# A hybrid decoder step with a mixture of experts: rows of second and third expert blocks move without a branch

## The chip, the cores and the metric

One core of a Trainium2 chip runs the whole program. The metric is device microseconds of one execution; a time that is told without more is the median of several runs. Times inside an execution come from a profile of one execution and count from the start of its span.

## The reference

Two trunk layers run over 512 prompt tokens and 64 sample tokens (8 sequences of 8), width 1024. Each layer has a mixer of three recurrences (GLA, retention, SSD) between two projections, a layer norm, and then a mixture of experts, which is where the change lies:

```python
p_group = softmax(t @ w_group + b_group)          # 4 groups
g_sel = argmax(p_group)
e_logits = (t @ w_expert + b_expert)[group g_sel]  # 4 experts in a group
top_v, top_i = top_k(e_logits, 2)
w_top = softmax(top_v) * p_group[g_sel]
hid = silu(t @ w1[e]) * (t @ w3[e])                # 256 wide, 16 experts
y = sum over e of w_top[e] * (hid @ w2[e])
```

Every token has two experts out of sixteen, so a layer has 2 x 576 = 1152 rows to send through experts. How many an expert gets depends on the data, and the kernel must be right for any split.

## The kernel before, in words

**The stage.** In each layer `phase_b` ends with the routing, and `experts` (L1819) then takes the sixteen experts in sixteen *turns*, `b` = 0 to 15, most crowded expert first in rank; the list `RANK` (L34) says which rank is taken in which turn. Every turn's expert gets a main block. A turn is *light* (`LIGHT`, L36: turns 0, 1, 3, 4, 6, 7, 9) when 64 rows are expected to do: class `Light` (L1392) gathers 64 rows and multiplies in plain float32. The other turns have a `Block` (L1307) of up to 128 rows, whose weights and rows are split in two parts (`split`, L323; L328 on ScalarE, L329 on VectorE; L1340, L1341 for the rows) for three products each.

**A block** is: `gather` (L1320, an indirect DMA on GpSimd's queue that fetches the rows of its tokens from `hbuf` by the indices in `srci`; an index past the end, 2047, fetches nothing), `turn` (L1329, eight transposes L1334), `up` (L1343, products L1353, SiLU L1355, L1357), `hid` (L1360), `down` (L1366, products L1373, written to a `ys` tile) and `scatter` (L1379, an indirect DMA L1384 on GpSimd's queue that writes the rows to `ybuf`). In a light block the lines are L1417, L1425, L1434 and L1442.

**More rows than a block has.** An expert of a non-light turn with more than 128 rows has a second block (`b2`), with more than 256 a third (`b3`); a light turn with more than 64 rows has a second light block (`bx`), and above 128 and 256 whole blocks on top; what lies above 384 rows goes through left-over blocks ahead of the turns (L1965, `nx` of them). `counts` (L1202) works this out on VectorE and writes numbers and bit masks to a small tile `ebi`; `values_load` (L1930) puts four of them (`nx`, `second`, `third`, `beyond`) in registers of every engine, and `tc.If` makes a branch on all engines. The body of an `If` is scheduled as one piece. A body that is skipped is replaced by instructions that bring the semaphores to where the body would have left them: an event semaphore on each engine and, where the body holds DMAs of GpSimd's queue, a counter step for these.

**Order of the turns.** The loop at L1988 runs 17 times. In turn b TensorE does `up` of block b, `turn` of block b + 1, `down` of block b - 1 and `hid` of block b. Between them stands one `If` per turn (L2009) on all the cases "at hand", and in it one for each case (`two`, L1906; `three`, L1908): in turn b - 1 the gather of b's second block (L2050), in turn b its transposes, up products and hidden rows (L2035 to L2040) with those of the third block, whose gather is there too, and in turn b + 1 its down products and scatter. The case of a light turn stands whole in its own turn (L2020 to L2032). Fifteen of the seventeen turns have such an `If`. Scatters of the non-light blocks have a branch of GpSimd alone that takes 64 or all rows (`parts`, L1934; L1938), and the gather of turn 9 is put ahead of its turn's branch (`GSPLIT`).

Weights come in pieces of 1 MB (`load`, L1915; DMA L1286 on SyncE's queue), three experts deep; a piece is asked for when the expert that held its room is through. Between the turns GpSimd also normalizes the residual rows (`aside`, L1848; L1854, L1855), once per turn in turns 2 to 6.

Of the kernel before, what the change touches and what calls it, by code (L numbers as in the profile page):

```python
# [9 lines left out]
F32 = mybir.dt.float32  # L10
# [28 lines left out]
ROWS = [min(128, 2 * T // max(r - 1, 1)) for r in RANK]  # L39

HALF = [64 if r > 80 else r for r in ROWS]
GSPLIT, SSPLIT = (9,), tuple(range(NE - 2))
SECOND = [b for b in range(NE) if RANK[b] < 2 + 2 * T // 129]
SOON = (2,)
THIRD = [b for b in range(NE) if RANK[b] < 2 + 2 * T // 257]
# [19 lines left out]
def _tables():  # L65
# [60 lines left out]
    put("pow2", np.tile(2.0 ** np.arange(16), (128, 1)))  # L126
    put("iota256", np.tile(np.arange(256.0), (128, 1)))
# [33 lines left out]
def _body(nc, tc, a, ctx, dbg):  # L161
# [1040 lines left out]
    def counts(tp, R, tabs, perm, count):  # L1202
# [189 lines left out]
    class Light(Block):  # L1392
# [27 lines left out]
        def up(self):  # L1420
# [76 lines left out]
    def phase_b(l, gates, nrm, gst, slots, rqk, rv, x, R, tabs, rst, fill):  # L1497
# [23 lines left out]
        R["iota"] = rp.tile([128, 481], F32, name="iota")  # L1521
        sp.dma_start(R["iota"], a["consts"][:, nres:nres + 481])
# [296 lines left out]
    def experts(last, finish, l, x, R, tabs, slots, rqk, rv, ahead):  # L1819
# [8 lines left out]
        with ExitStack() as sE:  # L1828
# [19 lines left out]
            def aside(b):  # L1848
                if 2 <= b < 2 + NT:
# [3 lines left out]
                    with tc.issue_after(bl[max(k for k in range(min(b + 3, NE)) if k not in GSPLIT)].got.ins):  # L1853
                        pool.tensor_tensor(xt, xt, ln1[:n, 0], op=ALU.mult)  # L1854
                        pool.tensor_tensor(xt, xt, ln1[:n, 1], op=ALU.add)  # L1855
# [36 lines left out]
            def take(t):  # L1892

                n = tp_(t)
                if t not in ys:
# [4 lines left out]
            bx = {b: light(b, Xx[b % 2], psx, 1, yss[3]) for b in LIGHT}  # L1900
            b2 = {b: Block(NE + b, tabs, scat, Xx[b % 2], xf if b in LIGHT else xs, hids[2], yss[3], sl2, psx, plain=b in LIGHT) for b in SECOND}
            b3 = {b: Block(2 * NE + b, tabs, scat, Xx[(b + (b in SOON)) % 2], xf if b in LIGHT else xs, hids[3], yss[(b + 2) % 3], sl2, psx, plain=b in LIGHT)
                  for b in THIRD}

            def two(b):
                return tc.If((beyond & (1 << b)) > 0)  # L1906

            def three(b, f):  # L1908
                if b in THIRD:
                    with tc.If((third & (1 << b)) > 0):  # L1910
                        f()
# [450 lines left out]
```

## Time and profile before

| | |
|---|---|
| median of 3 runs | 1481.08 us (1478.7 to 1485.45) |
| the profiled execution | 1481.09 us |
| its span, first to last instruction | 1479.3 us |
| granted TensorE clock, mean over the span | 0.918 of full speed |
| TensorE busy (matmul) | 1243.2 us, 84% |
| VectorE, ScalarE, GpSimd busy | 816.6, 488.1, 430.4 us (55, 33, 29%) |
| DMA | 267.45 MB, 181 GB/s over the span |
| experts' stage, layer 0 / layer 1 | about 475 to 700 us / 1165 to 1435 us |

An engine's busy time counts only work of the engine itself: branches, register loads, semaphore steps and the issuing of DMAs are not in it. A row of waits says which engine's instruction waited, for what, how long in all, how many times and the longest. "PEq L2009" as the reason means that TensorE's own instruction sequencer was at line 2009, a branch; "issue" means that the profile shows nothing it waited for. "PEldq" in the rows on branches is the same sequencer.

### The profile page before, as it was taken

The numbers are of one execution on the slowest core, as the hardware profiler recorded it, in microseconds if no ns is written. First come the engines' busy times: TensorE is split into PE (matmuls) and PEld (weight loads), VectorE is DVE, ScalarE is ACT, GpSimd is POOL, SyncE is SP. The second block draws the span as 40 slices with busy tenths as digits, with TensorE's granted clock in tenths as the row PEclk, the third lists the DMA queues.
The fourth block names the chain that finished last, engine by engine and source line by source line (L and its number), as shares of the span: only waits on it lengthen the run. The fifth ranks groups of instructions, "written<-read, shape, count | busy, mean of one in ns | idle before, by whom it ended". The sixth has DMA issues, their size and how long they took to land. (4 is left out here: it accounts for less than half of the span.)

```text
span 1479.3 us, 22669 instructions
## 1 busy us (share of the span) xinstructions
PE 1243.2 (84%) x8166; PEld 939.3 (63%) x8166; DVE 816.6 (55%) x1905; ACT 488.1 (33%) x902; POOL 430.4 (29%) x356
## 2 busy tenths in 40 slices
PE   4999999998985685999899998889997478558993
PEld 0998677675763454576589887777576355435761
DVE  0566457446888230366768647336789623022657
ACT  0552133321353221454454223323145223122522
POOL 0014112224153461221242322133324365112115
PEclk9999999999986797999999999999997689789997
DMA  8545666755152746796615310027544273572862
GB/s 293 184 144 164 221 228 212 279 203 184 66 170 91 259 171 230 288 404 240 191 65 171 88 58 33 29 63 271 172 161 136 107 290 124 231 275 95 346 204 90
DMA packets 96018, 267.45 MB, mean 181 GB/s; under 512 B 26263, under 2 KB 54841, under 8 KB 76920
## 3 DMA queue, kind: packets, MB, share of 16 engines
q1 hardware_dynamic: 84600, 246.60, 47.5%
q0 software_dynamic: 11264, 18.87, 3.8%
q8 instruction: 88, 1.44, 0.4%
q14 instruction: 66, 0.54, 0.1%
HBM read 238.43 MB, written 39.24 MB: 188 GB/s over the span
## 5 line engine op out<-in xcount | busy, mean ns | idle before, releaser
L402 PE MATMUL ps<-whi,hT 128*128 128x256 f32 (+1 forms) x640 | 189.9, 297 | 1.8 <-ACT hT L493 1.0
L404 PE MATMUL ps<-whi,hT 128*128 128x256 f32 (+1 forms) x640 | 184.1, 288 | 1.8 <-DVE hT L494 1.7
L403 PE MATMUL ps<-wlo,hT 128*128 128x256 f32 (+1 forms) x640 | 184.4, 288 | 0.7 <-DVE wlo L329 0.7
L402 PEld LDWEIGHTS ps<-whi,hT 128*128 128x128 f32 (+1 forms) x640 | 118.8, 186 | 15.1 <-issue 10.4
L403 PEld LDWEIGHTS ps<-wlo,hT 128*128 128x128 f32 (+1 forms) x640 | 118.5, 185 | 3.4 <-issue 2.1
L404 PEld LDWEIGHTS ps<-whi,hT 128*128 128x128 f32 (+1 forms) x640 | 118.5, 185 | 3.2 <-DVE hT L494 2.4
L392 PE MATMUL ps<-hT,whi 128*128 128x288 f32 x512 | 88.6, 294 | 0.0
L329 DVE TENSOR_TENSOR wlo<-wraw,whi 128x2048 fp32r<-128x2048 f32 x30 | 68.6, 2288 | 33.3 <-ACT whi L328 33.1
L1341 DVE TENSOR_TENSOR xl<-ps,xh 128x512 fp32r<-128x512 f32 x48 | 31.2, 684 | 89.6 <-ACT xh L1340 84.1
L265 PE MATMUL ada<-wada,scond 128*32 128x512 f32 x384 | 58.1, 678 | 21.0 <-DMA wada<-w_ada 21.0
L392 PEld LDWEIGHTS ps<-hT,whi 128*128 128x128 f32 x512 | 74.7, 188 | 0.4 <-ACT zdt L531 0.4
L1562 PE MATMUL ps<-whi,mh 128*128 128x512 f32 (+1 forms) x160 | 70.9, 443 | 3.7 <-ACT mh L1548 3.7
L329 DVE TENSOR_TENSOR wlo<-w3rd,whi 128x2048 fp32r<-128x2048 f32 x22 | 55.2, 2507 | 30.9 <-ACT whi L328 29.7
L1564 PE MATMUL ps<-whi,ml 128*128 128x512 f32 (+1 forms) x160 | 68.3, 431 | 3.8 <-DVE ml L1549 3.8
L1563 PE MATMUL ps<-wlo,mh 128*128 128x512 f32 (+1 forms) x160 | 70.1, 438 | 0.0
L1353 PE MATMUL ps<-whi,xh 128*128 128x256 f32 x384 | 58.9, 298 | 7.6 <-DVE xl L1341 7.6
L328 ACT ACTIVATE whi<-wraw 128x2048 fp32r<-128x2048 f32 x30 | 57.3, 1911 | 19.4 <-PE ps L392 7.7
L842 POOL TENSOR_TENSOR qh<-qx,ex 128x256 f32<-128x256 f32 x32 | 31.3, 1007 | 99.2 <-issue 83.5
L1373 PE MATMUL ps<-w3rd,hid 128*128 128x512 f32 x128 | 58.1, 596 | 2.2 <-DVE ys L1377 2.2
L1353 PEld LDWEIGHTS ps<-whi,xh 128*128 128x128 f32 x384 | 51.6, 199 | 11.5 <-DVE xl L1341 11.0
L1322 POOL DMA_INDIRECT qk<-hbuf,srci x22 | 22.7, 1033 | 121.6 <-PE ps L1417 70.0
L1384 POOL DMA_INDIRECT ybuf<-ys,srci x20 | 27.5, 1375 | 104.4 <-ACTq L2009 33.9
(552 smaller groups left out, 2937.5 us busy)
## 6 DMA issues: line engine op xcount, KB each, us to landing
wada<-w_ada SPq DMA_DIRECT2D x48, 1024.0 KB
wraw<-moe_w SPq DMA_DIRECT2D x36, 1024.0 KB
slots<-moe_w SPq DMA_DIRECT2D x30, 1024.0 KB
w3rd<-moe_w SPq DMA_DIRECT2D x30, 1024.0 KB
wraw<-w_in SPq DMA_DIRECT2D x22, 1024.0 KB
wraw<-w_out SPq DMA_DIRECT2D x8, 1024.0 KB
ybuf<-bz SPq DMA_DIRECT2D x8, 512.0 KB
hbuf<-g SPq DMA_DIRECT2D x8, 512.0 KB
```

The costliest lines, as they stand in the source:

```text
L265: pe.matmul(acc[32 * q:32 * q + 32, :], sc_[:, k, :], w[:, o:o + 512], start=(k == 0), stop=(k == KD - 1))
L328: split.hi = act.activation(hi[:, :n], raw[:, :n], AF.Copy)
L329: dve.tensor_tensor(lo[:, :n], raw[:, :n], hi[:, :n].bitcast(F32), op=ALU.subtract)
L392: pe.matmul(p[:mw, :], lhs[:, k, m0:m0 + mw], rhs[:, k, 288 * h:288 * (h + 1)], start=(k == 0 and lhs is vh and rhs is hT[0]), stop=(k == ...
L402: pe.matmul(p[:n], hT[0][:, k, xs], vh[:, k, :], start=(k == 0), stop=False)
L403: pe.matmul(p[:n], hT[0][:, k, xs], vl[:, k, :], start=False, stop=False)
L404: pe.matmul(p[:n], hT[1][:, k, xs], vh[:, k, :], start=False, stop=(k == KD - 1))
L1353: pe.matmul(p, x[:, k], v[:, k], start=(x is self.xh and v is vh and k == 0), stop=(x is self.xl and k == KD - 1))
L1373: pe.matmul(p, self.hT[:, f], v[:, f, c], start=(f == 0), stop=(f == 1))
L1562: pe.matmul(p[:n], mh[:, k, :n], vh, start=(k == 0), stop=False)
L1563: pe.matmul(p[:n], mh[:, k, :n], vl, start=False, stop=False)
L1564: o = pe.matmul(p[:n], ml[:, k, :n], vh, start=False, stop=(k == 3))
```

## The change

Second and third blocks of the non-light turns (`MORE`: turns 2, 5, 8, 10, 11, 12, 13; a third block in turns 2, 5, 8, 13) are gathered and scattered in any case, outside of any branch; where an expert has too few rows for them, all their indices are past the end. A second block is gathered two turns ahead of its own, a third one turn ahead, and both are scattered in their own turn. Only their products (`extra`) stand behind a branch: one on b's bit, and in it one on the third's. All of a block's work, its down products too, is now in its own turn. The cases of light turns go out of the turns: they stand, with the left-over blocks, in one branch ahead of the loop, which loads its weights itself. One register, `flags`, holds all bits; the others are loaded inside that branch. The extra gathers use two X tiles in turn, `ys` tiles that could be read unwritten are zeroed by VectorE, and the 64-row scatters and the special place of turn 9's gather are gone. Small edits of tables (`pow3`, the width of `iota` and `ebi`) are left out here.

```diff
+MORE = [b for b in SECOND if b not in LIGHT]
+LIGHTS, NXS, THIRDS = sum(1 << b for b in LIGHT), 16, {b: 19 + i for i, b in enumerate(b for b in THIRD if b not in LIGHT)}
...
-        dve.scalar_tensor_tensor(j[:, 3], p, float(min(HALF[:NE - 2])), R["iota"][0:1, 465:481], op0=ALU.is_gt, op1=ALU.mult, accum_out=b[:, 3:4])
         dve.tensor_tensor(j[:, 0], p, R["iota"][0:1, 449:465], op=ALU.is_gt)
-        dve.scalar_tensor_tensor(j[:, 0], j[:, 0], 1.0, R["iota"][0:1, 465:481], op0=ALU.mult, op1=ALU.mult, accum_out=b[:, 4:5])
-        dve.tensor_copy(tabs[2][:, NX + 19:NX + 21], b[:, 3:5])
+        dve.scalar_tensor_tensor(j[:, 0], j[:, 0], 1.0, R["iota"][0:1, 465:481], op0=ALU.mult, op1=ALU.mult, accum_out=b[:, 3:4])
+        dve.scalar_tensor_tensor(j[:, 3], p, 256.0, R["iota"][0:1, 481:497], op0=ALU.is_gt, op1=ALU.mult, accum_out=b[:, 4:5])
+        dve.scalar_tensor_tensor(b[:, 3:4], b[:, 0:1], 2.0 ** NXS, b[:, 3:4], op0=ALU.mult, op1=ALU.add)
+        dve.tensor_tensor(tabs[2][:, NX + 19:NX + 20], b[:, 3:4], b[:, 4:5], op=ALU.add)
...
+            b2, b3, k = {}, {}, 0
+            for b in SECOND:
+                for i, d in enumerate((b2, b3)):
+                    if i == 0 or b in THIRD:
+                        d[b] = Block((1 + i) * NE + b, tabs, scat, Xx[k % 2], xf if b in LIGHT else xs, hids[2 + i], yss[3] if i == 0 else yss[(b + 1) % 3],
+                                     sl2, psx, plain=b in LIGHT)
+                        k += 1
...
-            nx, second, third, beyond = [nc.values_load(tabs[2][0:1, i:i + 1], min_val=0, max_val=m)
-                                         for i, m in ((NX, NX), (NX + 1, 2 ** NE - 1), (NX + 2, 2 ** NE - 1), (NX + 20, 2 ** NE - 1))]
-            half = pool.value_load(tabs[2][0:1, NX + 19:NX + 20], min_val=0, max_val=2 ** NE - 1)
+            flags = nc.values_load(tabs[2][0:1, NX + 19:NX + 20], min_val=0, max_val=2 ** 23)
+
+            def bit(i):
+                return tc.If((flags & (1 << i)) > 0)
+
+            def extra(q, w):
+
+                q.w = w
+                q.turn()
+                for i in range(2):
+                    q.up(i)
+                q.hid()
+                q.down()
...
+            dve.memset(yss[3], 0.0)
+            dve.memset(yss[0][:, 512:], 0.0)
...
-            with tc.If(nx > 0), ExitStack() as sI:
+            with tc.If((flags & (LIGHTS | 7 << NXS)) > 0):
+                for b in LIGHT:
+                    with bit(b):
+                        e = sp.value_load(tabs[2][0:1, NX + 3 + b:NX + 4 + b], min_val=0, max_val=NE - 1)
+                        for i in range(3):
+                            expert_piece(l, e, i, w3rd[i])
+                        whole(bx[b], w3rd)
+                        if b in SECOND:
...
+                nx = nc.values_load(tabs[2][0:1, NX:NX + 1], min_val=0, max_val=NX)
+                wr = w3rd[0]
+                with tc.If(nx > 0), ExitStack() as sI:
...
-                if b + 3 in GSPLIT:
-                    parts(b + 3, bl[b + 3].gather, True)
-
-                at_hand = [e for e in (b - 1, b, b + 1) if e in SECOND and e not in LIGHT or e == b and b in LIGHT]
...
-                with tc.If((beyond & sum(1 << e for e in at_hand)) > 0) if at_hand else nullcontext():
-                    if b - 1 in at_hand:
-                        with two(b - 1):
-                            b2[b - 1].down()
-                            b2[b - 1].scatter()
...
-                    if b in at_hand and b in LIGHT:
-                        with two(b):
...
-                    elif b in at_hand:
-                        with two(b):
-                            b2[b].turn()
-                            if b not in SOON:
-                                three(b, lambda: b3[b].gather())
-                            b2[b].up(0)
-                            b2[b].up(1)
-                            b2[b].hid()
...
-                    if b + 1 in at_hand:
-                        with two(b + 1):
-                            b2[b + 1].gather()
...
+                if b in MORE:
+                    with bit(b):
+                        extra(b2[b], bl[b].w)
+                        if b in THIRD:
+                            with bit(THIRDS[b]):
+                                extra(b3[b], bl[b].w)
...
                 if b + 1 < NE:
                     bl[b + 1].turn()
-                    if b + 3 < NE and b + 3 not in GSPLIT:
+                    if b + 3 < NE:
                         bl[b + 3].gather()
+
+                    for e, d in ((b + 1, b3), (b + 2, b2)):
+                        if e in MORE and e in d:
+                            d[e].gather()
...
-                    st = parts(b - 1, bl[b - 1].scatter, b - 1 in SSPLIT)[0]
+                    st = bl[b - 1].scatter()
+                    for d in (b2, b3):
+                        if b in MORE and b in d:
+                            d[b].scatter()
```

## Rows read from the trace of the kernel before

**Rows 1.** The page, busy us (share of the span) and instructions of TensorE

```profile
PE 1243.2 (84%) x8166; PEld 939.3 (63%) x8166; DVE 816.6 (55%) x1905; ACT 488.1 (33%) x902; POOL 430.4 (29%) x356
```

**Rows 2.** By stage: length, PE PEld DVE ACT POOL busy (instructions), clock, DMA share, GB/s

```profile
475.00:700.00 225.00, 183.82 (x1105) 125.57 (x1106) 86.64 (x109) 76.15 (x105) 72.71 (x50) 0.91 0.70 262
1165.00:1435.00 270.00, 209.81 (x1243) 143.97 (x1244) 88.41 (x117) 77.73 (x113) 77.36 (x52) 0.89 0.58 215
```

**Rows 3.** Waits of TensorE, stage of layer 0: us in total, times, longest

```profile
PE ps L1334 <- DMA X<-hbuf,srci: 13.6, 1, 13.6
PE ps L1334 <- PEq L2020: 5.7, 1, 5.7
PE ps L1417 <- PEq L2009: 5.2, 1, 5.2
PE ps L1442 <- PEq L2020: 3.4, 3, 1.4
```

**Rows 4.** Waits of TensorE, stage of layer 1

```profile
PE ps L1334 <- DMA X<-hbuf,srci: 29.2, 2, 15.4
PE ps L1417 <- PEq L2009: 4.9, 1, 4.9
...
PE ps L1442 <- PEq L2020: 4.1, 4, 1.7
...
PE ps L1334 <- PEq L2020: 1.7, 1, 1.7
```

**Rows 5.** Timeline of GpSimd around 560 us: start, us, instruction, idle before

```profile
555.58 1.03 POOL L1384 DMA_INDIRECT ybuf<-ys,srci  x1 [0.17 <-issue]
566.11 1.02 POOL L1322 DMA_INDIRECT X<-hbuf,srci  x1 [9.50 <-issue]
```

**Rows 6.** GpSimd's sequencer at L2020, 555.6 to 566 us

```profile
L2020 POOLq COMPARE_BRANCH  x1: 45/45/45, 555.7 to 555.7; - x1
L2020 POOLq EVENT_SEMAPHORE  x1: 17/17/17, 564.6 to 564.6; - x1
```

**Rows 7.** Timeline of TensorE, 573 to 588 us

```profile
575.15 1.94 PE L1334 MATMUL ps<-cst,X 128*128 128x128 f32 x8 [13.55 <-DMA X<-hbuf,srci]
577.70 2.07 PE L1353 MATMUL ps<-whi,xh 128*128 128x256 f32 x8 [0.61 <-DVE xl L1341]
...
581.97 1.11 PE L1353 MATMUL ps<-whi,xh 128*128 128x256 f32 x8
```

**Rows 8.** Source lines L1322: gathers into the X tiles, ns min/median/max

```profile
L1322 POOL DMA_INDIRECT X<-hbuf,srci x6: 1004/1028/1033, 502.4 to 1320.1; - x6
```

**Rows 9.** Timeline of TensorE, transposes elsewhere in the stage

```profile
601.10 1.09 PE L1334 MATMUL ps<-cst,v 128*128 128x128 f32 x8
```

**Rows 10.** Table by stretch, columns as in rows 2: just after the X wait

```profile
575.00:581.00 6.00, 5.24 (x24) 4.87 (x25) 1.38 (x2) 1.20 (x2) 0.00 (x0) 0.53 0.04 14
```

**Rows 11.** TensorE's sequencer at L1965, branch of the left-over blocks, both layers

```profile
L1965 PEldq COMPARE_BRANCH  x2: 3860/4164/4467, 487.2 to 1175.1; - x2
```

**Rows 12.** Flag loads of TensorE's sequencer at L1930, ns min/median/max

```profile
L1930 PEldq TENSOR_LOAD <-ebi x8: 300/308/497, 486.6 to 1179.9; - x8
```

**Rows 13.** TensorE's sequencer at L2009 in turn 0 of layer 0

```profile
L2009 PEldq COMPARE_BRANCH  x1: 1929/1929/1929, 493.2 to 493.2; - x1
```

**Rows 14.** All branches of TensorE's sequencer at L2020 and L2009

```profile
L2020 PEldq COMPARE_BRANCH  x15: 170/218/6783, 501.6 to 1364.2; - x15
...
L2009 PEldq COMPARE_BRANCH  x30: 68/148/2428, 493.2 to 1410.6; - x30
```

**Rows 15.** Timeline of TensorE: down products of the last turn, idle before

```profile
693.54 3.70 PE L1373 MATMUL ps<-wraw,hid 128*128 128x512 f32 x8 [0.47 <-ACT hid L1364]
```

**Rows 16.** Source line L1384: scatters, ns min/median/max

```profile
L1384 POOL DMA_INDIRECT ybuf<-ys,srci x20: 973/998/3036, 544.3 to 1418.8; - x20
```

**Rows 17.** Groups of GpSimd: normalized rows, busy and mean ns, idle before

```profile
L1855 POOL TENSOR_TENSOR x<-x,slots 128x1024 f32<-128x1024 f32 (+1 forms) x10 | 29.5, 2948 | 0.8
...
L1854 POOL TENSOR_TENSOR x<-x,slots 128x1024 f32<-128x1024 f32 (+1 forms) x10 | 23.7, 2367 | 0.2
```

More of the change, by code (lines that the diff above doesn't have):

```diff
@@ L126, in _tables @@
     put("pow2", np.tile(2.0 ** np.arange(16), (128, 1)))
+    put("pow3", np.tile([2.0 ** THIRDS[b] if b in THIRDS else 0.0 for b in range(NE)], (128, 1)))
     put("iota256", np.tile(np.arange(256.0), (128, 1)))
@@ L1418, in turn, with up @@
             act.activation(self.xT, p.rearrange("p (k n) -> p k n", k=KD), AF.Copy)
-        def up(self):
+        def up(self, i=0):
             v = [w.rearrange("p (k n) -> p k n", k=KD) for w in self.w[:2]]
@@ L1520, in phase_b @@
         pool.tensor_copy(R["ur"][:, 1], ones)
-        R["iota"] = rp.tile([128, 481], F32, name="iota")
-        sp.dma_start(R["iota"], a["consts"][:, nres:nres + 481])
+        R["iota"] = rp.tile([128, 497], F32, name="iota")
+        sp.dma_start(R["iota"], a["consts"][:, nres:nres + 497])
         wm = rp.tile([128, KD, 2, 20], F32, name="wm")
@@ L1852, in aside @@
                     act.activation(xt, xt, AF.Identity, scale=st[:, 1:2], bias=st[:, 2:3])
-                    with tc.issue_after(bl[max(k for k in range(min(b + 3, NE)) if k not in GSPLIT)].got.ins):
+                    with tc.issue_after(bl[min(b + 2, NE - 1)].got.ins):
                         pool.tensor_tensor(xt, xt, ln1[:n, 0], op=ALU.mult)
@@ L1897, in take @@
                 loads[t] = [sp.dma_start(ys[t][:n, k], ybuf[PL * k + 128 * t:PL * k + 128 * t + n]) for k in range(2)]
[L1900 to L1911, printed above, removed]
+            bx = {b: light(b, Xx[0], psx, 1, yss[3]) for b in LIGHT}
+            b2, b3, k = {}, {}, 0
[5 more added lines that the diff above has]
+                        k += 1
             ids = {0: 0, 1: 1}
@@ L1929, in experts @@
                 pool.memset(ln1[:, i, 0:1], 0.0)
-            nx, second, third, beyond = [nc.values_load(tabs[2][0:1, i:i + 1], min_val=0, max_val=m)
-                                         for i, m in ((NX, NX), (NX + 1, 2 ** NE - 1), (NX + 2, 2 ** NE - 1), (NX + 20, 2 ** NE - 1))]
-            half = pool.value_load(tabs[2][0:1, NX + 19:NX + 20], min_val=0, max_val=2 ** NE - 1)
-            def parts(b, f, both):
-                h, r = HALF[b], ROWS[b]
-                if b not in LIGHT and h < r and both:
-                    with tc.If((half & (1 << b)) > 0) as big:
-                        o = [f(slice(0, r))]
-                    with big.Else():
-                        o.append(f(slice(0, h)))
-                    return o
-                return [f(slice(0, r))]
+            flags = nc.values_load(tabs[2][0:1, NX + 19:NX + 20], min_val=0, max_val=2 ** 23)
[8 more added lines that the diff above has]
+                q.down()
             def whole(q, w):
@@ L1949, in whole @@
                 q.turn()
-                for i in range(2):
+                for i in range(1 if isinstance(q, Light) else 2):
                     q.up(i)
```

74 lines of the change are left out of this document (24 added, 50 removed).

## The prediction

> **What bounds the kernel now.** I read the busy lines first: TensorE is the busy engine [rows 1]. The change touches one stage that runs once per layer, the sixteen turns of the experts, so next comes the table by stage: in the first layer's stage (225 us) TensorE is busy 183.8 us, in the second's (270 us) 209.8, and there the DMA engines stand at 0.70 and 0.58 and GpSimd works 73 and 77 us [rows 2]. So TensorE sets the pace, and some 41 and 60 us of its idle time are what can be won. Third, the waits of TensorE in these stretches [rows 3, 4]. Nearly all are of two kinds: "DMA X", a wait for the gathered rows of a second block (13.6 us once, 29.2 us in two), and "PEq", where TensorE's own sequencer stood in a branch (L2009, L2020).
>
> Why the rows of X come late is seen on GpSimd's queue. It issues a scatter at 555.58 and the X gather at 566.11, with nothing between [rows 5]. In between its sequencer leaves the untaken branch of a 64-row block (L2020) in 45 ns at 555.7, and the next thing it does is a semaphore wait that is over at 564.6 [rows 6]. As I read it, a skipped body that holds GpSimd transfers has to step the counters of the transfers left out, and that waits until an earlier scatter has landed, 9 us after its issue. Only then comes the gather, and its rows need 9.0 us more (566.11 to 575.15 [rows 5, 7]).
>
> **The change, part by part.** Rows in the trace show six extra blocks: six X gathers [rows 8], two in the first layer, four in the second. Their products are in both kernels.
>
> (1) *Gathers out of the branches, two turns ahead (a second block) or one (a third).* GpSimd's list has no counter to step between the turns any more. A gather issued a turn or two ahead of a product that PE reaches 12 us or more per two turns later covers the 9.0 us landing. Gone: 13.6 + 29.2 = 42.8 us. What is late next in turn 5 is the block's down weights: issued a turn before and behind them PE still has some 9 us of the extra block's own up products, so I charge nothing; if that cover were missing it would cost up to the rest of one landing, 9 us, kept for the upper end.
>
> (2) *Clock after these waits.* Right after the wait the eight transposes took 1.94 us against 1.09 elsewhere, the first eight products 2.07 against 1.11 a few lines later [rows 7, 9], and the granted clock of that stretch is 0.53, so mostly the lower of its two levels, after 13.55 us in which TensorE did nothing [rows 7, 10]. 0.85 + 0.96 = 1.8 us, three times: 5.4 us gone.
>
> (3) *Branch of turn 0.* TensorE waits 5.2 and 4.9 us [rows 3, 4]. In that time it skips the left-over blocks (branch of 4.47 and 3.86 us, partly under earlier products [rows 11]), loads three more flags (0.31 us each [rows 12]) and skips the 64-row case of turn 0 (1.93 us [rows 13]). The first stays, now over a longer body; the flags become one, the last goes. 1.93 + 3 x 0.31 = 2.9 us in the first layer; for the second I take 2.6, its wait being 0.3 shorter. 5.5 us. Bounds: if the longer skip costs the dearest branch in the trace, 6.78 us [rows 14], instead of 4.2, it eats 2 x 2.6 = 5.2, so this part is worth 0.3 to 5.5.
>
> (4) *Branch of turn 1.* The skip of its 64-row case, with two whole blocks inside it, is that 6.78 us branch; TensorE waited 5.7 and 1.7 us on it. 7.4 us gone.
>
> (5) *Skips of 64-row cases in later turns* (3, 4, 6, 7, 9): "ps L1442 from PEq L2020", 3.4 and 4.1 us [rows 3, 4]: 7.5 us gone.
>
> (6) *The seven branches left in each layer.* Their bodies are about what the outer branch of such a turn skips now; the 30 of L2009 have a median of 0.15 us and a worst of 2.43 [rows 14]. They are run ahead of the array, so I charge 0; bounds 0 to 14 x 2.43 = 34 us (the worst row in all), and I stay near the median.
>
> (7) *Down products inside the branch.* Today an extra block's down products run a turn later, with its hidden rows long ready. Now they follow directly and wait for them, as in the last turn: 0.47 us [rows 15]. Six times: 3 us added, bounds 0 to 6.
>
> (8) *GpSimd.* 11 gathers and 11 scatters per layer in any case are 44, against 12 today: 32 more at 1.0 us each [rows 8, 16], 18 in the first stage, 14 in the second. GpSimd would work 91 us in each. Nothing waits for it as long as its list of a turn is shorter than the turn; I charge 4 us for a scatter that comes a little late and holds a ys tile (a guess; bounds 0 to rival A). On the DMA engines the absent rows have indices past the end and are dropped; even if all moved, 32 x 0.5 MB are 43 us at 262 / 0.70 = 374 GB/s [rows 2], in room that lies idle.
>
> (9) *Counting, flag arithmetic, two memsets on VectorE, full instead of half scatters, fewer flag loads on SP:* a handful of instructions beside TensorE's work in the head of the stage; the flags are needed only after the transposes of turn 0. 0.
>
> Sum: 42.8 + 5.4 + 5.5 + 7.4 + 7.5 - 3 - 4 = 61.6, or 62 us. The profiled execution took 1481.1 us (span 1479.3), the median of the runs shown is 1481.1 too: 1481 - 62 = **1419 us** (-4.2%).
>
> **Rivals.**
>
> A: *GpSimd falls behind, and the X wait comes back as a wait for its list.* In turns 2 to 6 it also carries the normalized rows, 2.4 + 2.9 us a turn [rows 17]. Turns 2 to 5 have 4, 3, 3 and 4 transfers; 3.5 at 1.0 us and these make 8.8 us, under the 12.5 us of a turn (200 us over 16). But the same scatter has taken up to 3.04 us [rows 16]: at that price 3.5 x 3.04 + 5.3 = 16 us a turn, 3.5 too much in four turns of two layers: 28 us, 1447 us. Against it: the median is 1.0. [...] 0.16.
>
> B: *Other waits fill the place,* the weights above all: TensorE goes through the stage 30 us faster with the same 48 MB. Half of (1) and (2) comes back: 24 us, 1443 us. Against it: DMA share 0.70 and 0.58 [rows 2]. 0.10.
>
> C (slower): *every skip of a second block fetches its code.* A block of the second kind with its third is some 260 TensorE instructions to jump over; (4) shows such a jump at 6.78 us, (3) at 3.86 to 4.47. Place: the 14 branches, on TensorE's sequencer. Price n each: 14 n - 62 us; it decides from n = 4.4 us, and at 5.5 gives +15, 1496 us. Against it: median 0.15 [rows 14]. [...] 0.04.
>
> D: *the change does not do what it says:* the early gathers still wait on GpSimd, for their X tile to be freed in the branch two turns before, and land as late. (1) and (2) stay, 48 us: 1467 us. 0.03.
>
> **How the numbers follow.** The forecast itself has 0.67 with 1400 to 1435 (costs in (7), (8) at zero and some clock won at the head of the stage; or (3) at 0.3, one landing in (1)). The range takes in A and B, 1398 to 1450; C, D and the far ends are left out. About 0.5%, 7.4 us, is what a measurement of this kernel can tell. Faster: forecast, A, B, most of D, 0.94; same 0.03; slower 0.03.
>
> **What would show it.** Right: no "DMA X" among TensorE's waits; X gathers two turns ahead of their transposes, GpSimd with 76 + 32 transfers; no branch wait in turn 1; stages near 200 and 235 us; no half-clock stretch in mid-stage. Wrong: TensorE waiting for xh or ys behind a scatter's landing or GpSimd at work without gaps (A); DMA share near 1 with waits for weights (B); branches of microseconds at the seven skips (C); X waits as before (D).

## The result and the profile after

| | before | after |
|---|---|---|
| median, lowest to highest | 1479.89 us (1478.64 to 1485.45, 4 runs) | 1433.81 us (1431.05 to 1434.84, 4 runs) |
| profiled execution, its span | 1481.09, 1479.3 us | 1432.89, 1431.1 us |
| GpSimd instructions | 356 | 388 |
| experts' stage, layer 0 / layer 1 | 217.7 / 262.4 us | 203.8 / 230.1 us |

The change makes the kernel faster: the ratio is 0.968, 95% interval 0.965 to 0.971, or 46 us where 62 were forecast; 1434 lies in the range. A stage is counted here from the first transposes of turn 0's rows (L1417 before, L1419 after) to the end of the last down product (L1373, L1375). Of the 48 us by which the span is shorter, 13.9 are in the first stage and 32.4 in the second, and the first one starts 3.7 us earlier; 1.7 are lost again outside of the two. In the changed kernel the same code stands one to two lines lower in the file (L1384 is L1386 there, L329 is L330).

TensorE's waits after, by line and reason: total, how many, the longest. First the stage of layer 0 (475 to 680 us), beside [rows 3]:

```profile
PE ps L1355 <- ACT xh L1342: 6.3, 2, 3.3
PE ps L1355 <- DVE wlo L330: 5.0, 1, 5.0
PE ps L1355 <- DVE xl L1343: 4.3, 4, 2.0
PE ps L1419 <- PEq L1963: 2.2, 1, 2.2
...
PE ps L1375 <- ACT hid L1366: 1.4, 3, 0.5
```

then that of layer 1 (1152 to 1383 us), beside [rows 4]:

```profile
PE ps L1355 <- ACT xh L1342: 6.3, 2, 3.3
PE ps L1355 <- DVE xl L1343: 5.9, 6, 1.8
PE ps L1355 <- DVE wlo L330: 4.4, 2, 3.1
...
PE ps L1375 <- ACT hid L1366: 2.4, 5, 0.5
PE ps L1419 <- PEq L1963: 2.0, 1, 2.0
```

No wait for "DMA X" is left, nor one for a branch in turn 1 or in a later 64-row turn; turn 0's branch (now L1963) costs 2.2 and 2.0 us. In their place stand waits that the kernel before does not have: for the split rows (their first part is xh, the second xl) and for the split weights (whi and wlo). They stand in two places. The first is turn 2; TensorE, VectorE and GpSimd there, from three timelines of the changed kernel (start, duration, instruction, and in brackets the idle time before it and what ended it):

```profile
504.18 2.08 PE L1355 MATMUL ps<-wlo,xh 128*128 128x256 f32 x8 [4.96 <-DVE wlo L330]
506.05 1.72 PE L1355 MATMUL ps<-whi,xl 128*128 128x256 f32 x8
507.61 1.11 PE L1355 MATMUL ps<-whi,xh 128*128 128x256 f32 x8
```

```profile
497.21 6.91 DVE L330 TENSOR_TENSOR wlo<-w3rd,whi 128x2048 fp32r<-128x2048 f32 x1 [1.18 <-ACT whi L329]
```

```profile
491.10 1.00 POOL L1324 DMA_INDIRECT X<-hbuf,srci  x1 [0.30 <-issue]
...
497.28 2.39 POOL L1857 TENSOR_TENSOR x<-x,slots 128x1024 f32<-128x1024 f32 x1
499.62 2.35 POOL L1856 TENSOR_TENSOR x<-x,slots 128x1024 f32<-128x1024 f32 x1
502.14 2.93 POOL L1386 DMA_INDIRECT ybuf<-ys,route  x1 [0.17 <-issue]
```

The split takes 6.91 us, and it lies beside two operations of GpSimd on the normalized rows: 2.29 us, what such a split takes elsewhere, and 2.39 and 2.35 make 7.03. The next one, 4.26 us from 505.36 on, lies beside most of a third (2.38 us from 505.08 on). TensorE waits 4.96 us and then runs at about half speed for a while (2.08 and 1.72 us, then 1.11; the granted clock from 503 to 508 us is 0.66). Before the change the same split took 2.29 us, and GpSimd stood idle beside it, from its X gather until TensorE had done the transposes behind turn 1's branch. VectorE and GpSimd in the kernel before:

```profile
505.82 2.29 DVE L329 TENSOR_TENSOR wlo<-w3rd,whi 128x2048 fp32r<-128x2048 f32 x1 [1.19 <-DMA wraw<-moe_w]
...
511.54 1.00 POOL L1322 DMA_INDIRECT v<-hbuf,srci  x1 [8.14 <-PE ps L1334]
```

The second place is turns 11 and 12. TensorE at the end of turn 10:

```profile
608.37 1.94 PE L1444 MATMUL ps<-wraw,hid 128*64 128x512 f32 x8
610.24 0.44 PE L1365 MATMUL ps<-cst,qk 128*128 128x128 f32 x2
613.96 2.07 PE L1355 MATMUL ps<-whi,xh 128*128 128x256 f32 x8 [3.28 <-ACT xh L1342]
615.83 2.04 PE L1355 MATMUL ps<-wlo,xh 128*128 128x256 f32 x8
...
630.29 2.08 PE L1355 MATMUL ps<-whi,xh 128*128 128x256 f32 x8 [3.06 <-ACT xh L1342]
```

and ScalarE:

```profile
610.36 0.69 ACT L1445 ACTIVATE ys<-ps,route 128x512 f32<-128x512 f32 x1 [5.33 <-PE ps L1444]
610.94 0.38 ACT L1366 ACTIVATE hid<-ps 128x256 f32<-128x256 f32 x1
611.51 1.91 ACT L329 ACTIVATE whi<-w3rd 128x2048 fp32r<-128x2048 f32 x1 [0.19 <-ACTq L2016]
613.33 1.07 ACT L1342 ACTIVATE xh<-ps 128x512 fp32r<-128x512 f32 x2
```

ScalarE idles 5.3 us, passes the untaken branch of turn 10 (L2016), and only then splits weights and rows of block 11, with TensorE waiting. The granted clock from 612 to 622 us is 0.66; in steps of half a microsecond it reads 1.00 up to 613.0 us, 0.50 from 613.5 to 620.0 and 1.00 again from 620.5 on:

```profile
612.00:622.00 10.00, 8.04 (x44) 7.98 (x45) 5.69 (x4) 4.58 (x5) 4.02 (x3) 0.66 0.97 377
```

(its columns: stretch, length, busy us with counts of PE, PEld, DVE, ACT, POOL, then granted clock, DMA share, GB/s).

The theory at this point: the forecast gains came, and two new waits took part of them back, one made by the order on ScalarE around an untaken branch, the other by GpSimd and VectorE in each other's way. The first half of this did not stand, as kernel 2 below shows.

### The profile page after: what moved, and what is told of

Same layout as the page of the kernel before. It is cut to its first block, busy times and chain, and to the rows that moved or that the text cites. A ratio compares the mean times of both kernels' runs of the same rounds, so it can differ in the third digit from the quotient of the medians.

```text
span 1431.1 us, 21969 instructions
## 1 busy us (share of the span) xinstructions
PE 1239.5 (87%) x8166; PEld 940.2 (66%) x8166; DVE 832.9 (58%) x1911; ACT 487.9 (34%) x902; POOL 478.3 (33%) x388
## 3 DMA queue, kind: packets, MB, share of 16 engines
q0 software_dynamic: 15872, 18.89, 4.0%
## 5 line engine op out<-in xcount | busy, mean ns | idle before, releaser
L1386 POOL DMA_INDIRECT ybuf<-ys,srci x36 | 46.9, 1302 | 132.5 <-issue 52.6
L330 DVE TENSOR_TENSOR wlo<-wraw,whi 128x2048 fp32r<-128x2048 f32 x30 | 68.6, 2287 | 34.5 <-ACT whi L329 34.1
L330 DVE TENSOR_TENSOR wlo<-w3rd,whi 128x2048 fp32r<-128x2048 f32 x22 | 67.7, 3078 | 24.3 <-ACT whi L329 23.1
L1355 PEld LDWEIGHTS ps<-whi,xh 128*128 128x128 f32 x384 | 52.5, 203 | 26.7 <-ACT xh L1342 13.6
L1355 PE MATMUL ps<-wlo,xh 128*128 128x256 f32 x384 | 59.8, 303 | 9.5 <-DVE wlo L330 9.4
L1355 PEld LDWEIGHTS ps<-wlo,xh 128*128 128x128 f32 x384 | 53.8, 208 | 12.4 <-DVE wlo L330 12.0
L329 ACT ACTIVATE whi<-wraw 128x2048 fp32r<-128x2048 f32 x30 | 57.3, 1910 | 12.5 <-PE ps L393 7.7
L1375 PE MATMUL ps<-w3rd,hid 128*128 128x512 f32 x128 | 58.6, 600 | 2.8 <-ACT hid L1366 2.8
```

The source lines that it names most:

```text
L329: split.hi = act.activation(hi[:, :n], raw[:, :n], AF.Copy)
L330: dve.tensor_tensor(lo[:, :n], raw[:, :n], hi[:, :n].bitcast(F32), op=ALU.subtract)
L1355: pe.matmul(p, x[:, k], v[:, k], start=(x is self.xh and v is vh and k == 0), stop=(x is self.xl and k == KD - 1))
L1375: pe.matmul(p, self.hT[:, f], v[:, f, c], start=(f == 0), stop=(f == 1))
```

## The experiments

All on one core, timed in several rounds beside the kernel before, whose median was 1482 us each time (1480 beside the changed kernel); "stages" are layers 0 and 1, counted as above, of the one profiled execution. That execution is the fastest of its kernel in 2 (1420.8 us) and 6 (1409.1) and the slowest in 3, 7 and 8 (1424.3, 1412.6, 1442.6), so stages of different kernels are compared with care.

| kernel | median (range), us | ratio to before, 95% | stages, us |
|---|---|---|---|
| after | 1433.8 (1431.0 to 1434.8) | 0.968 (0.965 to 0.971) | 203.8, 230.1 |
| 1 no late branches | 1395.9 (1391.6 to 1399.5) | 0.942 (0.938 to 0.946) | 190.0, 208.1 |
| 2 down and hid held back | 1431.1 (1420.8 to 1439.5) | 0.966 (0.963 to 0.969) | 195.5, 225.3 |
| 3 no GpSimd operations | 1419.9 (1416.1 to 1424.3) | 0.958 (0.954 to 0.961) | 196.3, 224.5 |
| 4 64-row cases in their turns | 1443.1 (1441.8 to 1446.3) | 0.974 (0.971 to 0.977) | 211.8, 235.9 |
| 5 64-row cases ahead, alone | 1421.6 (1418.5 to 1425.4) | 0.960 (0.958 to 0.962) | 197.1, 225.4 |
| 6 branch ahead of down | 1418.5 (1409.1 to 1423.3) | 0.958 (0.956 to 0.961) | 192.6, 221.4 |
| 7 = 6 + 8 | 1405.5 (1401.6 to 1412.6) | 0.947 (0.945 to 0.950) | 192.9, 219.2 |
| 8 operations later | 1440.6 (1428.4 to 1442.6) | 0.969 (0.965 to 0.974) | 206.5, 235.4 |
| 9 = 6, operations on VectorE | 1399.9 (1394.3 to 1402.6) | 0.946 (0.940 to 0.951) | 184.1, 212.1 |
| 10 = 5, one branch ahead | 1409.9 (1405.9 to 1416.5) | 0.954 (0.948 to 0.959) | 193.4, 216.0 |
| 11 = 10, operations on VectorE | 1402.9 (1398.3 to 1408.6) | 0.948 (0.943 to 0.954) | 188.3, 216.9 |

**1. The branches of turns 10 to 13 left out.**

```diff
-                if b in MORE:
+                if b in MORE and b < 10:
                     with bit(b):
                         extra(b2[b], bl[b].w)
```

> The changed kernel without the branches of turns 10 to 13 (the second and third products of these turns are left out; with these data none of them are run). Theory (order on ScalarE): where a branch is not taken it still cuts ScalarE's order, so that the split of block b+1's rows (xh) comes behind it, after ys and hid of earlier blocks; TensorE's waits for xh in turns 11 and 12 (3.28 and 3.06 us in layer 0, the same in layer 1) and the half-clock products after them go away: 3.2 + 3.1 + 2.0 of waiting and about 2 x 2.5 of slow products a layer, 15 to 20 us in all, so about 1415 to 1420 us against 1433. Rival (the waits come from late rows or from what these branches cost by themselves, or from an engine that is full there): waits of 3 us stay at the same places, and the time stays at 1430 to 1434.

38 us less, twice what was expected. In layer 0 the wait for wlo in turn 2 is as in the changed kernel (4.9 us), so all 13.9 us of that stage are those of the branches. In layer 1 the split of turn 2 happened to take 3.2 us this time, and no wait for wlo over 0.3 us stood there (4.4 us in the changed kernel); that is part of its 22 us. The end of turn 10, TensorE and then ScalarE:

```profile
613.94 0.44 PE L1365 MATMUL ps<-cst,qk 128*128 128x128 f32 x2
614.14 1.20 PE L1355 MATMUL ps<-whi,xh 128*128 128x256 f32 x8
```

```profile
608.63 1.91 ACT L329 ACTIVATE whi<-w3rd 128x2048 fp32r<-128x2048 f32 x1
611.64 1.91 ACT L329 ACTIVATE whi<-w3rd 128x2048 fp32r<-128x2048 f32 x1 [1.10 <-PE ps L1355]
613.45 1.07 ACT L1342 ACTIVATE xh<-ps 128x512 fp32r<-128x512 f32 x2
```

The splits stand ahead of ys and hid, and begin beside the up products of block 10. So untaken branches are dear, but why is still open.

**2. ScalarE's order restored, branches kept.** (`done` is the second copy of xh.)

```diff
+    with tc.issue_after(bl[b + 1].done.ins) if b in MORE and b + 1 not in LIGHT else nullcontext():
         bl[b - 1].down()
...
+    with tc.issue_after(bl[b + 1].done.ins) if b in MORE and b + 1 not in LIGHT else nullcontext():
         bl[b].hid()
```

> The changed kernel with all branches, but in turns with a second block the down products of block b-1 and the hidden rows of block b are held back until xh of block b+1 has been issued, so that ScalarE's order is again xh before ys and hid. Theory (order on ScalarE): the waits of 3.28 and 3.06 us for xh in turns 11 and 12 of both layers go as in the kernel without the branches, and the time is the same as that one's within 4 us (1415 to 1421), which would say that an untaken branch costs next to nothing by itself. Rival (branch itself): this stays at 1430 to 1434 while the kernel without branches is faster. A third case: holding back moves the wait to the hidden rows or the down products (TensorE waits for hid), then 1425 to 1433 with waits under other names.

My theory fell: the time stays at 1431, as the rival had it. xh does stand ahead of ys and hid now, and TensorE still waits 2.58 us. TensorE, then ScalarE:

```profile
603.97 1.22 PE L1355 MATMUL ps<-whi,xh 128*128 128x256 f32 x8 [2.58 <-ACT xh L1342]
```

```profile
601.52 1.91 ACT L329 ACTIVATE whi<-w3rd 128x2048 fp32r<-128x2048 f32 x1 [5.77 <-PEq L2016]
603.33 1.07 ACT L1342 ACTIVATE xh<-ps 128x512 fp32r<-128x512 f32 x2
604.29 1.92 ACT L329 ACTIVATE whi<-w3rd 128x2048 fp32r<-128x2048 f32 x1
606.09 0.69 ACT L1445 ACTIVATE ys<-ps,route 128x512 f32<-128x512 f32 x1
```

(The profiled execution is 10 us under the median; its wait for wlo in layer 0 was 1.2 us instead of 5.0, so its shorter stage there is not the work of this edit alone.) The reason now shows: ScalarE waited 5.77 us for "PEq L2016", TensorE's own passing of the branch. The body reads the split weights and rows of block 10, so their rooms come free for block 11 only when TensorE is through with the body or past it, and in TensorE's list the branch stands behind the hidden rows of block 10, as its last item before the up products of block 11. TensorE then has nothing left to do while 1.91 us of weights and 0.6 us of rows are split. The kernel before had the same rooms and the same kind of branch, but in turns 10 and 11 the branch stood ahead of the down products of block b - 1 and the hidden rows, so that some 4 us of products covered the splits. ScalarE and TensorE at that place in turn 11 of the kernel before:

```profile
645.88 1.91 ACT L328 ACTIVATE whi<-wraw 128x2048 fp32r<-128x2048 f32 x1 [3.30 <-PEq L2009]
...
646.04 3.60 PE L1373 MATMUL ps<-slots,hid 128*128 128x512 f32 x8
```

The new theory: it is the *place* of the branch in TensorE's order; the down products, now inside, made the body one piece that came to stand behind them (why it came to stand there is my reading).

**3. GpSimd's operations on the normalized rows left out.**

```diff
                     with tc.issue_after(bl[min(b + 2, NE - 1)].got.ins):
-                        pool.tensor_tensor(xt, xt, ln1[:n, 0], op=ALU.mult)
-                        pool.tensor_tensor(xt, xt, ln1[:n, 1], op=ALU.add)
+                        pass
```

> The changed kernel without GpSimd's two operations per turn that scale and shift the normalized residual rows (left out: the layer norm's scale and shift in the experts' stage). [...] Rival (late weights: the split is late since its weights or its room are late): the wait for wlo stays at 3 us or more and the time at 1429 to 1434.

I had expected the split of turn 2 back at 2.3 to 3.5 us and 1419 to 1424 us in all, and so it came, in rows and in time: 14 us less. All splits out of that room in the first stage, nanoseconds least, median, most:

```profile
L330 DVE TENSOR_TENSOR wlo<-w3rd,whi x12: 2280/2291/2294, 498.4 to 667.8; 128x2048 fp32r<-128x2048 f32 x12
```

against 2279/2293/6908 in the changed kernel, with the transfers still there. So it is the operations, not the 32 more transfers, that hold VectorE. The other kernels agree: in the stages of both layers every split over 2.6 us, before the change too (three, up to 4.1 us), lies beside one of these GpSimd operations, and kernels 3, 9 and 11, which have none there, have no such split.

**4. and 5. One half of the change at a time.** In 4 the rows move without a branch, but the 64-row cases stand in their turns; in 5 these stand ahead of the turns, and the rows of second and third blocks move inside the branches as before.

```diff
+                if b in LIGHT:
+                    with bit(b):
+                        whole(bx[b], bl[b].w)
...
-                for b in LIGHT:
-                    with bit(b):
-                        e = sp.value_load(tabs[2][0:1, NX + 3 + b:NX + 4 + b], min_val=0, max_val=NE - 1)
...
```

> The changed kernel with one part undone: the cases of the 64-row experts stand again each in its own turn behind a branch (with a small row tile of their own), while the rows of second and third blocks still move in any case. It tells how much of the gain belongs to which half. Theory: the branch waits come back (turn 1: 5.7 and 1.7 us, turn 0: about 2, the later 64-row turns 3.4 and 4.1: some 17 us) and, since GpSimd again steps its counters behind an earlier scatter in each of these turns, its list runs late by up to 9 us there; but the second blocks' rows were asked for two turns ahead, so that TensorE waits little or nothing for X: 1450 to 1460 us. Rival (the counter steps of GpSimd alone made the rows late, whatever the distance): waits for X of 5 to 13 us come back as well, 1465 to 1480 us.

```diff
+            with tc.If((beyond & sum(1 << e for e in LIGHT)) > 0):
+                for b in LIGHT:
+                    with two(b):
...
-                at_hand = [e for e in (b - 1, b, b + 1) if e in SECOND and e not in LIGHT or e == b and b in LIGHT]
+                at_hand = [e for e in (b - 1, b, b + 1) if e in SECOND and e not in LIGHT]
```

> The kernel before with the other half of the change alone: the cases of the 64-row experts stand in one branch ahead of the turns, while second and third blocks are still gathered and scattered inside the branches, a second block in the turn before its own. Theory (GpSimd's counter steps behind skipped 64-row cases made X late): with these skips out of the turns GpSimd reaches the gather of the taken turns 9 us earlier, TensorE's waits for X fall from 13.6 and 14.6 us each to 0 to 5 us, the branch waits of turn 1 and of the later 64-row turns are gone (14.9 us), those of turn 0 partly: about 1425 to 1445 us. Rival (a gather inside a branch one turn ahead is late by itself): the waits for X stay above 9 us each and only the branch waits go: 1460 to 1466 us.

Neither kernel has a wait of TensorE for X. In 4 the branch waits are back, these three in layer 0 (two) and layer 1:

```profile
PE ps L1419 <- PEq L2010: 5.5, 1, 5.5
PE ps L1336 <- PEq L2010: 5.3, 1, 5.3
...
PE ps L1419 <- PEq L2010: 5.9, 1, 5.9
```

and the time is 1443, better than the 1450 to 1460 that I gave it, in part since its waits for wlo are smaller (1.1 and 2.4 us). The surprise is 5: half of the change alone is 12 us *faster* than the whole, and faster than the 1425 to 1445 that I gave it. The X gathers stand in a branch one turn ahead as they always did, and are in time: GpSimd issued one at 494.0 us, its transposes began at 516.2. So what made X late before was the counter step behind the skipped 64-row case [rows 5, 6]. Kernel 5 takes that step out of the turns; kernel 4 leaves it there and asks early enough to cover it. The prediction's distance of two turns was not needed once the 64-row cases had gone. What 5 pays is at turn 0, where the two branches in a row (64-row cases, left-over blocks) hold TensorE 7 us in each layer:

```profile
PE ps L1417 <- PEq L1983: 7.0, 1, 7.0
...
PE ps L1417 <- PEq L1983: 7.2, 1, 7.2
```

**6. The branch ahead of the down products on TensorE.** `mm` is the last down product in the branch's body, `behind` lays an order of issue on TensorE's instructions alone.

```diff
                 if b > 0:
+                    k0 = len(nc.cur_bb.bb.instructions)
                     bl[b - 1].down()
+                    if b in MORE:
+                        behind(mm.ins, k0)
...
+                    k0 = len(nc.cur_bb.bb.instructions)
                     bl[b].hid()
+                    if b in MORE:
+                        behind(mm.ins, k0)
```

> The changed kernel with only TensorE's order altered: in a turn with a second block the branch stands ahead of the down products of block b-1 and of the hidden rows of block b, right behind the transposes of block b+1 (in the changed kernel it stands behind the hidden rows, next to the up products of block b+1, in turns 10 and 11). Everything is computed. Theory (place of the branch on TensorE): what the branch's body could read (the split weights and rows of block b) comes free only when TensorE has passed the branch; in turns 10 and 11 that is the last thing before the up products, so the split of the next weights (1.9 us) and of the rows (0.6 us) stand in the open. With some 4 us of down products and hidden rows behind the branch they are covered: the waits for xh of 3.3 and 3.1 us and the slow products after them go, as in the kernel without these branches (13.9 us in layer 0). The time is that kernel's plus a drain of at most 0.4 us for each of eight branches, and plus some 8 us where the wait for wlo in turn 2 of layer 1 is there: 1400 to 1412 us. Rival (a branch costs that much wherever it stands, by draining TensorE): waits of 2.5 us or more stay in turns 11 to 14, and the time at 1425 to 1434.

The waits for xh are gone but for one of 0.7 us. TensorE, then ScalarE, at the end of turn 10:

```profile
606.43 1.94 PE L1444 MATMUL ps<-wraw,hid 128*64 128x512 f32 x8 [0.30 <-PEq L2023]
608.30 0.44 PE L1365 MATMUL ps<-cst,qk 128*128 128x128 f32 x2
608.71 1.22 PE L1355 MATMUL ps<-whi,xh 128*128 128x256 f32 x8
```

```profile
606.26 1.91 ACT L329 ACTIVATE whi<-w3rd 128x2048 fp32r<-128x2048 f32 x1 [3.43 <-PEq L2023]
608.07 1.07 ACT L1342 ACTIVATE xh<-ps 128x512 fp32r<-128x512 f32 x2
```

The untaken branch costs 0.30 us here, and the splits lie beside down and hid. So the place of the branch is shown to be the cause of the waits for xh, and for these the rival (a branch costs that much anywhere) falls. It doesn't fall for every branch: in turn 13 of layer 1 TensorE waits for the untaken branch itself, longer than in the changed kernel (1.3 us there),

```profile
PE ps L1375 <- PEq L2023: 3.3, 1, 3.3
```

and in turn 8 of layer 0 it waits 1.3 us. The median, 1418, is 6 us above the range I gave. The other wait grew, with splits of up to 7.5 us and waits for wlo of 5.8 and 5.5 us in turn 2; but these rows are of an execution of 1409 us, inside the range, and what the slower ones lose isn't shown.

**8. and 7. GpSimd's operations later, alone (8) and with the branch ahead (7).** They follow the scatters of the extra blocks instead (`put2`).

```diff
-                if 2 <= b < 2 + NT:
-                    n, xt = tp_(b - 2), x[:tp_(b - 2), b - 2]
+                for t in {3: (0,), 5: (1, 4), 6: (2,), 8: (3,)}.get(b, ()):
+                    n, xt = tp_(t), x[:tp_(t), t]
...
-                    with tc.issue_after(bl[min(b + 2, NE - 1)].got.ins):
+                    with tc.issue_after(put2[-1].ins):
```

> The changed kernel with GpSimd's two operations on the normalized residual rows moved, not left out: they follow the scatters of the extra blocks, in turns 3 (one tile), 5 (two), 6 and 8 (one each) and no longer start in turn 2, where VectorE splits weights late. [...] Rival (GpSimd's work is too much in all): the wait goes to another place, a scatter or a gather that comes late behind these operations, and the time stays at 1428 to 1436.

> Both moves together: the branch ahead of the down products on TensorE, and GpSimd's operations on the normalized rows later. If the two waits have causes of their own and stand in different turns, the gains add up: 20 to 28 us from the first and 10 to 15 from the second, 1392 to 1402 us, which would be the fastest version here, the one without the late branches included (1396). If the gains share a cause or give way to a third wait: 1403 to 1412 us.

Alone, the move gained nothing (8: 1440.6, above the 1417 to 1424 us that I gave it and above the rival's range; its interval takes in that of the changed kernel). Turn 2 is mended, but two tiles' operations now meet the split of turn 7, VectorE and then GpSimd in kernel 8:

```profile
574.61 5.89 DVE L330 TENSOR_TENSOR wlo<-w3rd,whi 128x2048 fp32r<-128x2048 f32 x1 [1.62 <-ACT whi L329]
```

```profile
573.64 4.71 POOL L1858 TENSOR_TENSOR x<-x,slots 128x1024 f32<-128x1024 f32 x2
```

The collision moved with the operations. With the branch in its place the same move is worth 13 us (7 against 6), in the second of the cases that I gave. Why it is worth nothing without that wasn't followed further.

**9. The branch ahead, and the operations on VectorE,** in the 64-row turns (`gate` is VectorE's product of the up step).

```diff
-                if 2 <= b < 2 + NT:
+                if b in (3, 4, 6, 7, 9):
...
-                    with tc.issue_after(bl[min(b + 2, NE - 1)].got.ins):
-                        pool.tensor_tensor(xt, xt, ln1[:n, 0], op=ALU.mult)
-                        pool.tensor_tensor(xt, xt, ln1[:n, 1], op=ALU.add)
+                    with tc.issue_after(bl[b].gate.ins):
+                        dve.tensor_tensor(xt, xt, ln1[:n, 0], op=ALU.mult)
+                        dve.tensor_tensor(xt, xt, ln1[:n, 1], op=ALU.add)
```

> The changed kernel with the branch ahead of the down products on TensorE (as in the earlier run, 1418 us) and the two operations per tile on the normalized residual rows done by VectorE in the 64-row turns 3, 4, 6, 7 and 9 instead of by GpSimd. Everything is computed. [...] Rival (the dense scatters alone hold VectorE): splits of 4 us or more stay in turn 2, and the time at 1412 to 1420.

1399.9 us, inside the 1398 to 1406 us that I gave it, the fastest kernel here that computes everything, 34 us below the changed one. Its splits in the first stage (the one of turn 2, at 495.98 us, took 2.29 us):

```profile
L330 DVE TENSOR_TENSOR wlo<-w3rd,whi x12: 2281/2285/2292, 496.0 to 654.8; 128x2048 fp32r<-128x2048 f32 x12
```

**10. and 11. What moving the rows is worth by itself.** 10 puts the two branches of kernel 5 into one outer branch; the edit is shown against kernel 5, without the branch of the left-over blocks, which moves inside. 11 adds the operations on VectorE, with the edit of 9.

```diff
-            with tc.If((beyond & sum(1 << e for e in LIGHT)) > 0):
+            with tc.If(((beyond & sum(1 << e for e in LIGHT)) + nx) > 0):
...
```

> The kernel before with the cases of the 64-row experts moved ahead of the turns, as in the earlier run (1422 us), but that branch and the one of the left-over blocks stand in one outer branch, as they do in the changed kernel; rows of second and third blocks are still moved inside the branches of the turns. It asks what moving these rows without a branch is worth by itself. Theory (two branches ahead of turn 0 cost TensorE 7.0 and 7.2 us, one costs 2 to 2.5): 9 to 11 us less, 1410 to 1414 us, less than the changed kernel's 1434, so that moving the rows without a branch would be a loss of some 20 us by the place of the branch that came with it and the longer list of GpSimd. Rival (the time ahead of turn 0 is that of loading the flags): 7 us stay, 1419 to 1424.

> The kernel with one branch ahead of the turns and rows of second blocks inside the branches, and besides the operations on the normalized rows done by VectorE. Theory: its waits for wlo (4.6 and 3.1 us with two branches) go, 5 to 10 us less than with GpSimd's operations: 1402 to 1408 us. [...]

In 10 the wait at turn 0 falls to 2.9 and 2.7 us and the time to 1409.9, at the lower edge of what was expected. 11 is in its range (1402.9); the intervals of 10 and 11 overlap, so that the 7 us between them rest on the rows: in layer 0 no split takes over 2.3 us (4.9 in 10), and the waits for wlo are 1.5 us instead of 4.5. 9 and 11 differ in how the rows of second and third blocks move and in what came with it (down products a turn earlier, one register of flags, no 64-row scatters): 1399.9 and 1402.9 us, intervals 0.940 to 0.951 and 0.943 to 0.954. With these data, then, moving them without a branch is worth nothing that can be told here beside the other half, once both waits are mended. Alone each half ends the waits for X and has its gain: 39 us (kernel 4) and 60 us (kernel 5). The 34 us between the changed kernel and 9 are the place of the branch (15, kernel 6) and GpSimd's operations beside VectorE's splits (the other 19). What the 32 transfers cost by themselves wasn't tried alone.

## Why the prediction was right and where it was wrong

**The case forecast came, with a smaller sum.** By its steps:

- (1), (2) *X waits and the slow products behind them:* the waits are gone, all 42.8 us. The slow products behind them went too, but others came behind the new waits: for nearly the same number of products TensorE is busy 179.9 and 203.7 us in the two stages before and 179.8 and 201.5 after, so that of the 5.4 us of (2) about 2.4 are left. The cause read from [rows 5, 6] holds (kernel 5 takes the counter steps out of the turns and leaves the gather one turn ahead), but the remedy that I credited, the gather two turns ahead, is only one of two; I did not see that moving the 64-row cases would have done it alone.
- (3) *Turn 0:* 5.2 and 4.9 us became 2.2 and 2.0: 5.9 gained, 5.5 forecast. Kernels 5 and 10 show what it rests on: a second branch in a row costs 4.1 and 4.5 us.
- (4), (5) *64-row skips in the turns:* gone as forecast, 14.9 us.
- (6) *The branches left in each layer:* this is the step that failed. I charged 0, since an untaken branch takes TensorE's sequencer little time, and that is true of most of the 14 rows of L2016, least, median and most in ns:

```profile
L2016 PEldq COMPARE_BRANCH  x14: 76/221/3853, 513.4 to 1347.7; - x14
```

But I priced the branch and not what waits for it. Its body is a reader of the split weights and rows, and it came to stand last in the turn. Kernel 1 shows 13.9 us in layer 0 alone and 22 us in layer 1, where 4.1 us less of waiting for wlo are in it. That is near the bound of 34 us that I had from [rows 14], for another reason than I gave.
- (7) *Down products in the branch:* the waits for hid are 1.4 and 2.4 us with those that were there, six new ones at 0.47, 2.8 us; 3 forecast.
- (8) *GpSimd:* 32 more transfers, as counted, and no wait of TensorE is for one of them; their queue (q0 on the page) moved 18.89 MB where it had moved 18.87, so the absent rows moved next to nothing. In place of the 4 us charged for a late scatter came the wait for wlo, which I had not foreseen: 5.0 and 4.4 us and the slow products, 14 us by kernel 3.
- (9) nothing shows in the rows.

That 1434 lies in the range, and even in the forecast's own 1400 to 1435, is partly luck: (6) was too low by some 30 us and (8) by 10, but the gains were larger than the sum had them. Kernel 1, without eight of the nine branches that are not taken, is 86 us faster than the kernel before, 24 more than the 62 forecast, though its layer 0 still waits for wlo. TensorE's busy time in its stages is 174.3 and 194.5 us, 15 us under that of before, where (2) had 5.4: slow products stood behind more waits than those for X.

**Rival A** was half right, with the roles changed. It had GpSimd falling behind with transfers of 3 us. Such transfers came, 17 of 2.4 to 3.1 us in the two stages against 8 of 2.2 to 3.0 before, each begun while a split of VectorE ran; but no wait of TensorE is for one. What cost time is that GpSimd ran its operations of [rows 17] into VectorE's split in turn 2, and it was the split that took longer. Before the change GpSimd had been held there by the transposes behind turn 1's branch, the 5.7 us that (4) took away: the split came 8.6 us earlier than before (505.82 to 497.21), the first operation on the second tile of rows 13.0 us (512.57 to 499.62) and the last one on the first tile only 2.6 (499.87 to 497.28), so that both now fall beside the split. The 6.91 us of the split are about its 2.29 us and the 2.39 and 2.35 us of the two operations beside it, and with no such GpSimd operation in the turn it is 2.29 (kernels 3 and 9). Why a split takes longer beside them isn't shown.

**Rival B** in its form, late weights, did not come: no wait of TensorE is for weights, though the DMA share of the first stage rose to 0.78 and stands at 0.97 in the stretch shown.

**Rival C** did not come with its price, 4.4 us at every skip, but dear ones are there, which the median of 0.22 us hides. Nine of the 14 branches are not taken. The three of them whose body holds a third block (turns 8 and 13 of layer 0, turn 13 of layer 1) took TensorE's sequencer 0.34, 1.15 and 3.85 us, the other six 0.22 to 0.36. TensorE waited 1.3 us for the last one in the changed kernel, 3.3 in kernel 6 and 3.0 in kernel 9; in kernel 6 it waited 1.3 us for the first of the three, too. What makes these dear isn't shown: that a skip fetches its code was an assumption of the rival, and no run tested it.

**Rival D** did not come: X was issued at 491.1 for transposes at 515.6.

In layer 0 the gains of [rows 3] with turn 0's were to be 13.6 + 1.8 + 3.0 + 5.7 + 3.4 = 27.5 us; the stage won 13.9. The four largest new waits there are 4.96, 3.28, 3.06 and 1.97 us, 13.3 in all, which is about the difference. It isn't a full account: the slow products behind these waits and smaller waits that went are not in it.

## What to carry to other kernels

A branch that wasn't taken cost its place: the split weights and rows that its body could read stayed held until TensorE had passed it (ScalarE waited 5.77 us for that in kernel 2, and the earlier place was worth 15 us in kernel 6), so it should stand early in the turn, with independent work behind it on the engine that paces the kernel. When a stall is taken from an engine off the critical path, ask what it runs into next: GpSimd's idle time (8.14 us at that place) had kept its operations out of VectorE's way. And of a change with two halves run each alone; here the half that seemed the main one was worth nothing beside the other.

## What was not expected of the hardware

- A VectorE split of 2.29 us took 6.91 us, and 7.45 in kernel 6, beside two GpSimd operations on the normalized rows (2.39 and 2.35 us, 2.38 and 2.34 in kernel 6), that is, about its own time and theirs; the GpSimd operations at that place kept their 2.4 us, though the split of kernel 6 had begun 0.6 us ahead of the first. Elsewhere it was GpSimd that took longer: 4.32 us instead of 2.36 for one of them, at 504.76 us in kernel 5.
- TensorE's sequencer was at an untaken branch early, and its signal came only with the end of the products ahead of it: in the changed kernel it compared at 608.8 and 623.6 us (turns 10 and 11), the products ended at 610.68 and 627.23, and the signals came at 610.7 and 627.3. In kernel 6 the products ahead of turn 10's branch ended at 606.13 us, and ScalarE's split that waited for the signal began at 606.26. TensorE idled 0.30 us there, with other work behind the branch; where the splits of the next block had to wait for that signal and nothing else was left, it idled 2.6 us (kernel 2) to 3.3 (the changed kernel).
- The 3.3 us waits are followed by products at the lower clock (2.07, 2.04 us and so on against 1.11; granted clock 0.66 from 612 to 622 us), so such a wait costs more than its row says: the up products of turns 11 and 12 took 8.7 and 7.6 us against 6.5 and 6.0 without the late branches, 2.2 and 1.6 us on top of 3.28 and 3.06.
